# The recurrence gate's product dealt out between the attention's blocks, in a one-layer hybrid diffusion trunk

## The chip, the cores and the metric

One core of a Trainium2 chip runs the kernel. The time is device microseconds of one launch, the median of several runs. Lower is better.

## The reference

The reference is one layer of a latent diffusion trunk: 1024 latent tokens and 256 context tokens, width 1024, all in float32. Only what matters around the change is shown.

```python
z_q, z_k, z_v, z_dec, z_og, z_f, z_rx, z_rg = jnp.split(zl, IN_SPLITS, axis=-1)   # zl = hl @ w_in
q, k, v, la_f, la_b = gla_prepare(z_q, z_k, z_v, z_dec, w_dec, b_dec)
o_f, _ = gla_scan(q, k, v, la_f, s_f)
o_b_rev, _ = gla_scan(rev(q), rev(k), rev(v), rev(la_b), s_b)
...
h_f, h_b_rev = rglru_bidir(u, w_rg_a, b_rg_a, w_rg_x, b_rg_x, rg_lam, hf0, hb0)
...
y_gla = gla_norm_gate(o_gla, z_og, g_gla)
y_f = fourier_mix(z_f)
y_rg = h_rg * jax.nn.gelu(z_rg.astype(jnp.float32))
```

The layer's input is normalized and modulated into `hl` (the modulation's rows come from `w_ada`). One projection `w_in` gives the inputs of three parallel mixers: a gated linear attention in both directions over four heads, a 2-D Fourier mixing of `z_f`, and a convolution with a bidirectional linear recurrence whose output is multiplied by gelu of `z_rg`. The change is about that last product, `z_rg = hl @ w_in[:, 2080:2336]`. Behind the mixers come an output projection and a SwiGLU feed-forward.

## The kernel before, in words

Every large product is made of three float32r matmuls (`mm3`, L82 to L86): operands are split into a high half (a cast on ScalarE, ACT, L91) and a low half (a subtraction on VectorE, DVE, L92), and high x high, high x low and low x high are added in PSUM. `hl` is kept transposed, as 16 tiles. A transposed product such as `z_q`, `z_f` or `z_rg` is made in blocks of 128 output columns and halves of 512 tokens; each half needs eight steps of the contraction, 24 matmuls of 128x512. `z_T` makes halves one after the other; `z_steps` (L779) makes one half as a generator that stops after every second step of the contraction, so that a half is four pieces of six matmuls.

The attention works on two pairs of heads, `p` = 0 and 1. For each pair `kt_begin` (L507) starts the copy of `kT` with its halves exchanged, by DMAs from ACT's queue; `gla_states` (L579) makes the exponentials of the decays, the scaled keys `Kt`, their transposes `k_tr` on TensorE (PE), the products `kv` and from them the chunk states `St` on DVE (the `tt` and `St` instructions); it returns the last transpose as `mid`. Then `gla_block` (L620) is called for eight blocks of 128 tokens: the products `attn` on PE, masked on DVE (`am`), the products `o` on PE, their squares on ACT (`jk`), a scale `orst` on DVE and its power `ors` on GpSimd (POOL), and the scaled result `on` on ACT. It returns the last `attn` matmul as a mark.

Between the blocks stand pieces of other products. `queue` holds generators; `fill(n, mark)` (L792) takes n pieces from it and places them behind `mark` on PE. Before the change the queue holds q of pair 1 (`q_steps`, two halves) and f (`f_steps`, two blocks of columns with two halves each). The blocks of pair 0 take two pieces each, `gla_states(1)` three, the blocks of pair 1 one each, the last ones what is left. `rg_ctx` (L670) and `rg_gates` (L686) make the recurrence's gates: small matmuls `gate_ps` on PE, tanh and exponentials on ACT. `rg_scan` ends them with a square root on ACT and scans on DVE.

Behind the attention `z_rg` (L851, called in L919 and L920) makes the gate's product in one go, 96 matmuls, and evicts each quarter with a gelu on ACT into the tiles `yfr`. Then come eight steps of `ada_row` (L921): loads of `ada_raw` from `w_ada`, each multiplied and added to the tile `ada_acc` on DVE (L711). The first of these calls also ends the row before (two matmuls `row_ps`, two DVE instructions) and clears the next `ada_acc` on POOL and loads `b_ada` into it. Then come the weights `w_og` (loads, cast, subtraction), the recurrence's second half, the Fourier mixing, and the product `zn` of `w_og`.

What sets the order of the work: each engine runs its own list in order. The lists are made at compile time by a scheduler that runs a model of the time and takes, on each engine, the first in program order of those that are ready. Two things bind it: `issue_after(mark)` places what follows behind the mark on the same engine, and `in_order` (L1456) ties the first writes of all tiles of a memory pool to program order:

```python
NPG = 43
...
    for x, y in zip(first, first[1:]):
        if x is not y:
            tc.add_manual_dep(y, x.name, DATA, reason="memory in program order")

    in_order(names["pg"])
    in_order(names["hp"])
```

`pg` is a pool of 43 pages of 128x1024 floats in SBUF. `hl` takes 16 of them; weights (raw, high and low), `kT`, `Kt`, `St`, `qT`, `qTs`, `zf`, `yfr`, `on`, the recurrence's `tr`, `ti`, `a`, `rgc`, and each `ada_raw` and `ada_acc` take one page a tile. A load into a page waits for the last use of the tile that had it. PSUM has four banks `mm`, used by the pieces (`z`), by `o` and by `zn`, and four banks `aux`, used by the rest.

Of the kernel before, what the change touches and what calls it, by code (L numbers as in the profile page):

```python
# [13 lines left out]
AF = mybir.ActivationFunctionType  # L14
ALU = mybir.AluOpType

P = 128
# [10 lines left out]
C_Q, C_K, C_V, C_DEC, C_OG, C_F, C_RX, C_RG = 0, 256, 512, 1024, 1056, 1568, 1824, 2080  # L28
# [10 lines left out]
def tile_trunk(ctx: ExitStack, tc: tile.TileContext, A: dict):  # L39
# [9 lines left out]
    def pg(shape=(P, 1024), dt=F32, name="pg"):  # L49
        t = pool.tile(list(shape), dt, tag="pg", bufs=NPG, name=name)  # L50
        names["pg"].add(t.name)
        return t
# [180 lines left out]
    def w_T(c0):  # L233
        return split(w_T_load(c0), (P, KB, P))
# [193 lines left out]
    for p in range(2):  # L428
        ps = mm("zkc")
# [149 lines left out]
    def gla_states(p):  # L579

        gs = [gla_exp(p, d) for d in range(2)]
        St[p] = [pg((P, 8, P), name="St") for _ in range(2)]
        kn = {}
        for q in range(2):
            for d in range(2):
                kn[q, d], mid = gla_kT(p, d, q)
        tp = [None] * 2
        for q in range(2):
            for d in range(2):
                tp[d] = gla_kv(p, d, q, kn[q, d], gs[d], tp[d])  # L590
        return mid
# [4 lines left out]
    def z_q(p, h):  # L596
        if h == 0:
            qT.append(pg(name="qT"))
            qTs.append(pg(name="qTs"))
        hs = slice(h * 512, (h + 1) * 512)  # L600
        z_T(w_q[p], lambda ps, h: S.mul(qT[p][:, hs], ps, 0.125), (h,))
        exchange(qTs[p][:, hs], qT[p][:, hs])
# [17 lines left out]
    def gla_block(p, n):  # L620
        cs = slice(n * P, (n + 1) * P)
        if n % 4 == 0:
            gla_q(p, n // 4)
        am = hp((P, 2, P), name="am")
        at = [aux("attn")[:, 0:256].rearrange("p (d i) -> p d i", d=2) for _ in range(2)]
        for d in range(2):
            for h in range(2):
                mark = PE.matmul(at[h][:, d, :], Kt[p][d][R[h], cs], qx[p][h ^ d][R[h], cs], start=True, stop=True)
        for h in range(2):
            V.tensor_mul(am[:, h, :], at[h][:, 0, :], wmask)  # L630
            V.copy_predicated(am[:, h, :], imask, at[1 - h][:, 1, :])
        o = mm("o")
        for h in range(2):
            oc = o[:, h * P:(h + 1) * P]
            PE.matmul(oc, qx[p][h][:, cs], St[p][h][:, n, :], start=True, stop=False)
            PE.matmul(oc, am[:, h, :], vN[p][n // 4][:, n % 4, h * P:(h + 1) * P], start=False, stop=True)
        ss = sm("oss", 2)
        jk = pool.tile([P, P], mybir.dt.bfloat16, tag="jk", bufs=1, name="jk")
        for h in range(2):
            S.activation(jk, o[:, h * P:(h + 1) * P], AF.Square, accum_out=ss[:, h:h + 1])  # L640
        r = rstd(ss, P, "ors", 2)
        if n % 4 == 0:
            on[p][n // 4] = pg((P, 4, 256), name="on")
        for h in range(2):
            S.mul(on[p][n // 4][:, n % 4, h * P:(h + 1) * P], o[:, h * P:(h + 1) * P], r[:, h:h + 1])
        return mark
# [23 lines left out]
    def rg_ctx():  # L670
        tr, ti, a = (pg((P, 4, TC), name="rgc") for _ in range(3))
        for b in range(2):
            for d in range(2):
                rg_gate(tr[:, 2 * b + d, :], uTc[:, b, :], b, d, 0, TC)
                rg_gate(ti[:, 2 * b + d, :], uTc[:, b, :], b, d, 1, TC)
                rg_decay(a[:, 2 * b + d, :], tr[:, 2 * b + d, :], b, d)
            tv = ti[:, 2 * b:2 * b + 2, :]
            V.scalar_tensor_tensor(tv, tv, 1.0, uTc[:, b:b + 1, :].to_broadcast([P, 2, TC]), op0=ALU.add, op1=ALU.mult)
        rg_input(a, tr, ti)
        for b in range(2):  # L680
            for d in range(2):
                av, tv = a[:, 2 * b + d, :], ti[:, 2 * b + d, :]
                V.tensor_tensor_scan(fl(av, d), fl(av, d), fl(tv, d), 0.0, op0=ALU.mult, op1=ALU.add)
                V.tensor_copy(h0[:, 2 * d + b:][:, 0:1], av[:, (0 if d else TC - 1):][:, 0:1])
# [9 lines left out]
    def rg_scan(blk, d, part):  # L694
        a, tr, ti = part
        rg_input(a, tr, ti)
        V.tensor_tensor_scan(fl(a, d), fl(a, d), fl(ti, d), h0[:, 2 * d + blk:][:, 0:1], op0=ALU.mult, op1=ALU.add)
        if d == 0:
            hR.append(a)
        else:  # L700
            V.tensor_add(hR[blk], hR[blk], a)
# [51 lines left out]
    def ada_step(n=1):  # L753
        for _ in range(n):
            next(row_steps, None)
# [36 lines left out]
    def fill(n, mark):  # L792

        with tc.issue_after(mark.ins):
            while n and queue:
                if next(queue[0], queue) is queue:
                    queue.pop(0)
                else:
                    n -= 1

    def q_steps(p, h):
        hs = slice(h * 512, (h + 1) * 512)

        def ev(ps):
            S.mul(qT[p][:, hs], ps, 0.125)
            exchange(qTs[p][:, hs], qT[p][:, hs])
        return z_steps(w_q[p], h, ev)

    def f_steps(blk, h):
        return z_steps(w_f[blk], h, lambda ps: S.copy(zf[blk][:, h * 512:(h + 1) * 512], ps))  # L810

    mid = gla_states(0)
    z_q(0, 0)
    gates = pg((P, 8, P), name="gates")
    load(gates, A["gates"])
    with tc.issue_after(mid.ins):
        z_q(0, 1)
    rg_ctx()
    w_f = [w_T(C_F)]
    qT.append(pg(name="qT"))  # L820
    qTs.append(pg(name="qTs"))
    queue += [q_steps(1, 0), q_steps(1, 1)]
    for n in range(4):
        fill(2, gla_block(0, n))
        ada_step(0)
    w_f.append(w_T(C_F + P))
    zf = [pg(name="zf") for _ in range(2)]
    queue += [f_steps(0, 0), f_steps(0, 1)]
    for n in range(4, 8):
        fill(2, gla_block(0, n))  # L830
    kt_begin(1)
    mid = gla_states(1)
    queue += [f_steps(1, 0), f_steps(1, 1)]
    fill(3, mid)
    part = rg_gates(0, 0)
    for n in range(2):
        fill(1, gla_block(1, n))
    rg_scan(0, 0, part)
    for n in range(2, 4):
        fill(1, gla_block(1, n))  # L840
    w_rg = [w_T(C_RG)]
    part = rg_gates(0, 1)
    for n in range(4, 6):
        fill(1, gla_block(1, n))
    rg_scan(0, 1, part)
    for n in range(6, 8):
        fill(9, gla_block(1, n))
    w_rg.append(w_T(C_RG + P))

    yfr = [pg((P, 4, 256), name="yfr") for _ in range(4)]  # L850
    def z_rg(blk):  # L851
        def ev(ps, h):
            for j in range(2):
                act(yfr[2 * h + j][:, 2 + blk, :], ps[:, j * 256:(j + 1) * 256], AF.Gelu_apprx_tanh)
        z_T(w_rg[blk], ev)

    def y_rg(blk):
        for j in range(4):
# [57 lines left out]
            V.tensor_add(yfr[2][:, blk, 2 - q::2][:, ::-1], yc[:, m], ys[:, m])  # L916
        V.tensor_copy(yfr[2][:, blk, 0:1], cc[:, 0:1])

    z_rg(0)  # L919
    z_rg(1)  # L920
    ada_step(8)  # L921
    w_og = [w_N([(C_OG, 256)])]
    for d in range(2):
# [616 lines left out]
```

## Time and profile before

| what | value |
|---|---|
| median of 3 runs | 1119.17 us (1117.54 to 1119.43) |
| the profiled execution | 1119.34 us |
| its span, first to last instruction | 1116.6 us |
| PE busy with matmuls | 1079.7 us |
| DVE busy | 794.5 us |
| ACT busy | 506.4 us |
| POOL busy | 46.8 us |
| mean granted TensorE clock | 0.994 |

The 2.7 us between the time and the span lie around the first and the last instruction. Times in the rows are microseconds from the start of the span. The attention of pair 0 runs from about 186 to 239 us, that of pair 1 from about 247 to 287, `z_rg` from 276 to 300, and the product `zn` of `w_og` begins at 303. In a timeline row stand the start, the duration, the engine, the line and operation, the tiles (out<-in), the shapes and the number of instructions put together; in brackets the engine's idle time ahead of it and what ended that. An engine with a q (ACTq, SPq) is its sequencer issuing DMAs. Matmuls overlap one another, so the time that one takes is read from the distance of the starts.

### The profile page before, as it was taken

How to read it: one execution, taken by the hardware profiler on the slowest of the kernel's cores; microseconds unless marked ns; L12 is line 12 of the kernel's file. 1: busy time of each engine (PE TensorE's matmuls, PEld its weight loads, DVE VectorE, ACT ScalarE, POOL GpSimd, SP SyncE). 2: the span in 40 equal slices, each digit the busy share in tenths (PEclk: the TensorE clock that was granted, in tenths of full speed). 3: DMA queues.
4: the chain of work that ended last, by engine and by line, in shares of the span. 5: the costliest groups of instructions: out<-in, count | busy, mean ns of one | idle time of the engine just before them, and what ended most of it. 6: DMA issues, size and time to landing. Idle time of an engine off the chain costs nothing.

```text
span 1116.6 us, 15349 instructions
## 1 busy us (share of the span) xinstructions
PE 1079.7 (97%) x5696; PEld 902.2 (81%) x5696; DVE 794.5 (71%) x1394; ACT 506.4 (45%) x953; POOL 46.8 (4%) x64
## 2 busy tenths in 40 slices
PE   5999998999999999979999999999999999999997
PEld 3799896776789888858888888888888888888886
DVE  4375798476687445488897767887776569958694
ACT  4362765456453377684233332234232238554251
POOL 1000000113000010010000000000000000000100
PEclk9999999999999999989999999999999999999999
DMA  9913312121637232234443324633331578767572
GB/s 297 300 38 96 122 39 58 43 58 38 207 96 259 62 113 77 87 101 123 141 151 105 103 95 152 225 93 106 117 110 57 174 253 312 248 218 242 176 272 75
DMA packets 133411, 157.49 MB, mean 141 GB/s; under 512 B 8396, under 2 KB 88788, under 8 KB 133336
## 3 DMA queue, kind: packets, MB, share of 16 engines
q1 hardware_dynamic: 119400, 127.68, 36.4%
q10 hardware_dynamic: 13936, 28.84, 7.3%
q8 instruction: 44, 0.72, 0.3%
q14 instruction: 31, 0.25, 0.1%
HBM read 125.56 MB, written 28.57 MB: 138 GB/s over the span
## 4 chain that ended last, share of the span: by engine, by line
PE 89%; ACT 4%; DVE 3%; DMA 1%; issue 1%; POOL 1%; DVEq 0%; POOLq 0%; ACTq 0%
PE prod L86 12%; PE prod L84 12%; PE prod L85 12%; PE dn L84 6%; PE dn L86 6%; PE dn L85 6%; PE z L84 3%; PE z L85 3%; PE z L86 3%; PE o_ps L86 3%; PE o_ps L84 3%; PE o_ps L85 3%; PE zn L85 3%; PE zn L86 3%; PE zn L84 3%
## 5 line engine op out<-in xcount | busy, mean ns | idle before, releaser
L85 PE MATMUL dn<-dr,dl 128*128 128x512 f32 (+1 forms) x319 | 121.9, 382 | 0.0
L86 PE MATMUL dn<-dr,dl 128*128 128x512 f32 (+1 forms) x319 | 121.9, 382 | 0.0
L84 PE MATMUL dn<-dr,dl 128*128 128x512 f32 (+1 forms) x319 | 118.8, 382 | 0.0
L84 PE MATMUL prod<-a,b_hi 128*128 128x512 f32 x176 | 69.9, 397 | 4.2 <-ACT b_hi L91 4.2
L85 PE MATMUL zn<-w_lo,hl 128*128 128x256 f32 (+1 forms) x256 | 73.7, 291 | 0.0
L84 PE MATMUL zn<-w_hi,hl 128*128 128x256 f32 (+1 forms) x256 | 73.4, 290 | 0.0
L86 PE MATMUL zn<-w_hi,hl 128*128 128x256 f32 (+1 forms) x256 | 73.4, 289 | 0.0
L85 PE MATMUL prod<-a,b_hi 128*128 128x512 f32 x176 | 69.5, 395 | 0.0
L86 PEld LDWEIGHTS dn<-dr,dl 128*128 128x128 f32 x319 | 60.0, 188 | 11.6
L84 PEld LDWEIGHTS dn<-dr,dl 128*128 128x128 f32 x319 | 60.0, 188 | 11.5
L85 PEld LDWEIGHTS dn<-dr,dl 128*128 128x128 f32 x319 | 60.0, 188 | 11.6
L86 PE MATMUL prod<-a,b_lo 128*128 128x512 f32 x176 | 68.7, 395 | 0.6 <-DVE b_lo L92 0.6
L85 PE MATMUL prod<-s,wb_hi 128*128 128x512 f32 x176 | 68.5, 389 | 0.0
L84 PE MATMUL prod<-s,wb_hi 128*128 128x512 f32 x176 | 68.5, 389 | 0.0
L86 PE MATMUL prod<-s,wb_lo 128*128 128x512 f32 x176 | 68.4, 389 | 0.0
L84 PE MATMUL z<-hl,w_hi 128*128 128x512 f32 x160 | 63.0, 419 | 3.2 <-DVE hl L205 2.1
L85 PE MATMUL z<-hl,w_hi 128*128 128x512 f32 x160 | 63.9, 400 | 0.0
L1234 ACT CAST dl<-h 128x512 fp32r<-128x512 f32 x77 | 47.8, 621 | 34.2 <-issue 20.5
L86 PE MATMUL z<-hl,w_lo 128*128 128x512 f32 x160 | 63.1, 395 | 0.0
L1235 DVE TENSOR_TENSOR dl<-h,dl 128x512 fp32r<-128x512 f32 x77 | 53.0, 688 | 13.8 <-ACT dl L1234 13.7
L1167 ACT CAST b<-wf_raw 128x512 fp32r<-128x512 f32 x22 | 13.7, 623 | 102.4 <-PE prod L86 50.0
L1191 ACT ACTIVATE c<-c 128x512 f32<-128x512 f32 x22 | 13.9, 633 | 85.9 <-DVE c L1190 82.8
(376 smaller groups left out, 2805.5 us busy)
## 6 DMA issues: line engine op xcount, KB each, us to landing
ada_raw<-in_w_ada SPq DMA_DIRECT2D x48, 512.0 KB, 6.1
h<-hd SPq DMA_DIRECT2D x77, 256.0 KB, 4.3
wd_raw<-in_w_down SPq DMA_DIRECT2D x77, 256.0 KB, 5.1
wf_raw<-in_w_gate SPq DMA_DIRECT2D x28, 512.0 KB, 3.8
hd<-c ACTq DMA_DIRECT2D x52, 256.0 KB, 2.1
wf_raw<-in_w_up SPq DMA_DIRECT2D x22, 512.0 KB, 4.2
wraw<-in_w_in SPq DMA_DIRECT2D x12, 512.0 KB, 4.0
wo_raw<-in_w_out SPq DMA_DIRECT2D x8, 512.0 KB, 5.8
```

What stands on the lines that cost most here:

```text
L84: PE.matmul(out, lh, rh, start=start, stop=False)
L85: PE.matmul(out, lh, rl, start=False, stop=False)
L86: return PE.matmul(out, ll, rh, start=False, stop=stop)
L1167: S.copy(hi, u[:, 4:8])
L1191: S.activation(c21, c21, AF.Silu)
L1234: S.copy(t[:, 0, :], raw)
L1235: V.tensor_sub(t[:, 1, :], raw, t[:, 0, :].bitcast(F32))
```

## The change

The gate's product becomes 16 pieces (`rg_steps`, two blocks of columns with two halves of four pieces), evicted by plain copies into `yfr`, and joins the queue. The pieces move up: four of q stand behind the first pair's `mid`, ahead of `rg_ctx`; every block takes two, `gla_states(1)` four, and the last block what is left. The tiles `zf`, `yfr` and the gate's weights are made earlier accordingly. The gelu is done over the copied values behind the attention, in four instructions of 128x512. The calls `ada_step(0)` among the blocks are removed. The diff:

```diff
+    def rg_steps(blk, h):
+        def ev(ps):
+            for j in range(2):
+                S.copy(yfr[2 * h + j][:, 2 + blk, :], ps[:, j * 256:(j + 1) * 256])
+        return z_steps(w_rg[blk], h, ev)
+
     mid = gla_states(0)
     z_q(0, 0)
     gates = pg((P, 8, P), name="gates")
     load(gates, A["gates"])
-    with tc.issue_after(mid.ins):
-        z_q(0, 1)
-    rg_ctx()
-    w_f = [w_T(C_F)]
     qT.append(pg(name="qT"))
     qTs.append(pg(name="qTs"))
     queue += [q_steps(1, 0), q_steps(1, 1)]
+    with tc.issue_after(mid.ins):
+        z_q(0, 1)
+    fill(4, mid)
+    rg_ctx()
+    w_f = [w_T(C_F)]
+    zf = [pg(name="zf") for _ in range(2)]
+    queue += [f_steps(0, 0), f_steps(0, 1)]
     for n in range(4):
         fill(2, gla_block(0, n))
-        ada_step(0)
     w_f.append(w_T(C_F + P))
-    zf = [pg(name="zf") for _ in range(2)]
-    queue += [f_steps(0, 0), f_steps(0, 1)]
+    queue += [f_steps(1, 0), f_steps(1, 1)]
     for n in range(4, 8):
         fill(2, gla_block(0, n))
     kt_begin(1)
     mid = gla_states(1)
-    queue += [f_steps(1, 0), f_steps(1, 1)]
-    fill(3, mid)
+    fill(4, mid)
+    w_rg = [w_T(C_RG)]
+
+    yfr = [pg((P, 4, 256), name="yfr") for _ in range(4)]
+    queue += [rg_steps(0, 0), rg_steps(0, 1)]
     part = rg_gates(0, 0)
     for n in range(2):
-        fill(1, gla_block(1, n))
+        fill(2, gla_block(1, n))
     rg_scan(0, 0, part)
+    w_rg.append(w_T(C_RG + P))
+    queue += [rg_steps(1, 0), rg_steps(1, 1)]
     for n in range(2, 4):
-        fill(1, gla_block(1, n))
-    w_rg = [w_T(C_RG)]
+        fill(2, gla_block(1, n))
     part = rg_gates(0, 1)
     for n in range(4, 6):
-        fill(1, gla_block(1, n))
+        fill(2, gla_block(1, n))
     rg_scan(0, 1, part)
     for n in range(6, 8):
-        fill(9, gla_block(1, n))
-    w_rg.append(w_T(C_RG + P))
-
-    yfr = [pg((P, 4, 256), name="yfr") for _ in range(4)]
-    def z_rg(blk):
-        def ev(ps, h):
-            for j in range(2):
-                act(yfr[2 * h + j][:, 2 + blk, :], ps[:, j * 256:(j + 1) * 256], AF.Gelu_apprx_tanh)
-        z_T(w_rg[blk], ev)
+        fill(9 if n == 7 else 2, gla_block(1, n))
...
-    z_rg(0)
-    z_rg(1)
+    for j in range(4):
+        act(yfr[j][:, 2:4, :], yfr[j][:, 2:4, :], AF.Gelu_apprx_tanh)
     ada_step(8)
     w_og = [w_N([(C_OG, 256)])]
```

## Rows read from the trace of the kernel before

**Rows 1.** The page's first part: busy us, share of the span, instructions.

```profile
PE 1079.7 (97%) x5696; PEld 902.2 (81%) x5696; DVE 794.5 (71%) x1394; ACT 506.4 (45%) x953; POOL 46.8 (4%) x64
```

**Rows 2.** Stretches: start:end, length; busy PE, PEld, DVE, ACT, POOL; clock, DMA, GB/s.

```profile
190.00:200.00 10.00, 6.73 (x28) 5.65 (x29) 8.29 (x17) 8.56 (x14) 0.00 (x0) 0.83 0.01 2
200.00:240.00 40.00, 40.00 (x243) 32.00 (x243) 20.45 (x56) 18.87 (x61) 6.49 (x7) 1.00 0.22 53
240.00:276.00 36.00, 33.18 (x203) 23.11 (x199) 27.07 (x68) 25.02 (x57) 7.06 (x7) 1.00 0.12 34
```

**Rows 3.** PE's timeline ahead of the first block's o.

```profile
191.21 0.46 PE L628 MATMUL attn<-la,Kt 64*128 64x128 f32 x2 [1.51 <-DVE tt L573]
...
192.34 0.49 PE L628 MATMUL attn<-qT,Kt 64*128 64x128 f32 x2 [0.45 <-DVE am L630]
...
194.66 0.77 PE L635 MATMUL o<-St,qT 128*128 128x128 f32 x2 [1.61 <-DVE St L559]
...
196.50 0.63 PE L85 MATMUL z<-hl,w_hi 128*128 128x512 f32 x1
```

**Rows 4.** PE's timeline, the last two matmuls of z_rg.

```profile
299.55 0.39 PE L85 MATMUL z<-hl,w_hi 128*128 128x512 f32 x1
299.77 0.39 PE L86 MATMUL z<-hl,w_lo 128*128 128x512 f32 x1
```

**Rows 5.** PE's timeline, waits from 240 to 277 us.

```profile
244.30 2.81 PE L653 MATMUL gate_ps<-uT,gates 128*128 128x512 f32 x6 [1.06 <-DVE tt L573]
...
268.04 0.49 PE L636 MATMUL o<-vN,am 128*128 128x128 f32 x2 [0.37 <-DVE am L631]
...
273.65 0.49 PE L636 MATMUL o<-vN,am 128*128 128x128 f32 x2 [0.42 <-DVE am L631]
...
276.25 0.50 PE L84 MATMUL z<-hl,w_hi 128*128 128x512 f32 x1 [1.02 <-ACT on L645]
```

**Rows 6.** The turn to pair 1: ACT's and PE's timelines, Kt's landing, its products.

```profile
221.79 0.58 ACT L810 COPY zf<-z 128x512 f32<-128x512 f32 x1
221.79 1.12 ACTq L231 DMA_DIRECT2D Kt<-kT  x2
...
231.96 1.03 PE L549 MATMUL k_tr<-cm,Kt 128*128 128x128 f32 x8
...
Kt<-kT ACTq DMA_DIRECT2D x4, 256.0 KB, 3.7
...
L534 DVE TENSOR_TENSOR Kt<-Kt,ek 128x512 f32<-128x512 f32 x4 | 2.7, 684 | 0.0
```

**Rows 7.** Weights of f and gate: DVE's and ACT's timelines, landing of wraw.

```profile
195.14 1.22 DVE L92 TENSOR_TENSOR w_lo<-wraw,w_hi 128x1024 fp32r<-128x1024 f32 x1
...
259.68 1.07 ACT L91 CAST w_hi<-wraw 128x1024 fp32r<-128x1024 f32 x1
...
DMA to landing us min/median/max: 3.7/4.0/9.9
```

**Rows 8.** Behind the attention: the timelines of SP, DVE and PE.

```profile
275.05 5.23 SPq L70 DMA_DIRECT2D ada_raw<-in_w_ada  x3
287.55 0.24 SPq L70 DMA_DIRECT2D ada_acc<-in_b_ada  x1
...
285.68 0.17 DVE L119 TENSOR_SCALAR orst<-oss 128x2 f32<-128x2 f32 x1 [1.23 <-ACT jk L640]
...
290.42 10.53 DVE L711 SCALAR_TENSOR_TENSOR ada_acc<-ada_raw,s,ada_acc 128x1024 f32<-128x1024 f32 x8
...
301.82 2.36 DVE L92 TENSOR_TENSOR w_lo<-wraw,w_hi 128x1024 fp32r<-128x1024 f32 x2 [0.88 <-ACT w_hi L91]
...
300.00 3.59 PE L653 MATMUL gate_ps<-uT,gates 128*128 128x512 f32 x8
303.03 1.04 PE L84 MATMUL zn<-w_hi,hl 128*128 128x256 f32 x4
```

**Rows 9.** SP's waits from 120 to 380 us: total, times, longest.

```profile
SPq L70 <- DVE ti L665: 16.1, 2, 12.6
```

## The prediction

> **What bounds the kernel now.** I read the page's first part, then the table of stretches, then PE's timeline through the attention, then the timelines of ACT, DVE and SP for what stands around it. The page gives PE 97% of the span [rows 1]. The stretches [rows 2] say where PE is not busy: from 190 to 200 us (6.73 of 10.00, at a mean granted clock of 0.83) and from 240 to 276 (33.18 of 36.00); from 200 to 240 it is full. So the change can win only what PE loses in such stretches, and the sum below is one of PE's gaps: closed, left, and new.
>
> The losses by row. Ahead of the first block PE waits 1.51, 0.45 and 1.61 us, and right behind the third wait a 512-column matmul shows 0.63 us [rows 3] where later ones show 0.39 [rows 4]: the lower of the clock's two levels, 1.2 GHz, after three waits in a row. A clock of 0.83 over 10 us [rows 2] costs 10 x 0.17 = 1.7 us. Together 3.57 + 1.7 = 5.3 us. In the second pair's attention PE waits 1.06, 0.37, 0.42 and 1.02 us [rows 5]: 2.9 us. All that is to be won is 8.2 us, 0.7%.
>
> **The change part by part**, against the profiled execution's own 1119.34 us (span 1116.6 and 2.7 around it; 0.2 above the median of 1119.17).
>
> Work. The 16 pieces are the 96 matmuls that z_rg runs from 276.25 to 299.77 [rows 4, 5], at 0.23 us apart some 22 us; none is removed. Queue and slots match: q, f and gate have 8 + 16 + 16 = 40 pieces, and the fills take 4 + 16 + 4 + 14 and the last 2. ACT gets eight copies of 128x256 more. The nearest row is the zf copy of twice the size, 0.58 us [rows 6], so at most 4.7 us, in an attention where ACT is busy 25 of 36 us [rows 2]. The gelu goes from eight halves to four wholes, no dearer: 4 x 0.58 = 2.3 us. Both are costed at nothing: no PE instruction waits for the copies but through a bank, and the gelus fall in a wait for loads (below); without that cover they would cost 2.3 us. ada_step(0) issues nothing, so its removal is free. The number of DMAs is unchanged.
>
> First gap. Four q pieces (24 matmuls, 5.5 us) now stand behind z_q(0,1), just where PE lost 5.3 us. But memory is given in program order, and qT, qTs of pair 1 now stand ahead of the rgc tiles: their eviction and two exchange DMAs come first on ACT's queue, so rg_ctx's chain on ACT starts some 5 us later, with everything that waits for its scratch pages. The first f weights are split by 195.14 + 1.22 [rows 7]. They had the two pages of w_q(0), which now go to qT and qTs; raw, hi and lo come instead from what gla_q and rg_ctx release, between 193 and 202 by my count, plus a load of 4.0, a cast of 1.07 and a subtraction of 1.22 [rows 7]: about 205. f pieces are wanted from the third block, about 203. Ends: 5.3 won, or nothing. I take **-3.4**, nearer the full win, as f would be some 2 us late.
>
> Second pair's gaps. Two pieces a block instead of one put 8 x 1.37 us more matmuls where 2.9 us of waits stand. Ends -2.9 and 0; **-2.6**, since the first pair's blocks, with two pieces each, run from 200 to 240 with PE full [rows 2].
>
> The turn between the pairs. Now the exchange into Kt of pair 1 is issued at 221.79, right behind the first zf copy on ACT, and the first transposes of it (k_tr) run at 231.96 [rows 6], with z pieces over these 10.2 us. In program order Kt's pages stand behind zf[0]. In the changed order zf[1] stands ahead of Kt, and it is written by f(1,0), the last piece of block 7; so exchange, exponentials, products and transposes begin when PE has run out of pieces, and the next four are placed behind the last k_tr. The chain alone: copy 0.58, issues 1.12, landing 3.7, two products of 0.68 [rows 6]: 6.8 us. Under it lie o products (four pairs a block, at most 0.49 each [rows 5]: 2.0) and, if the order puts them there, the matmuls of rg_gates(0,0) (3.6, as those at 300.00 [rows 8]). Ends 0 and 7, the last with the clock's fall; I take **+3.0**, between what is left with both covers (1.2) and with one (4.8).
>
> Behind the attention. What lies under z_rg? On DVE eight ada steps of 1.28 us without a break from 290.42, on SP b_ada at 287.55 and the loads behind it; only then come w_lo at 301.82 and the first zn at 303.03 [rows 8]. The last block's orst is at 285.68, so 17.4 us pass from there to zn, with 14 us of z over them and 3.0 of gates(1,0), from 300.00 [rows 8]. In the change z is over when block 7 is: its last two pieces stand right behind that block's attn. The chain of loads and DVE steps gets no shorter, and can't come much earlier, since each load takes a page: SP waits 16.1 us in two waits for DVE's last use of ti [rows 9]. I count pages, of 43: at block 5 of pair 1 the change holds hl 16, on 4, yfr 4, zf 2, w_rg 2, Kt 2, St 2, tr, ti and a 3, and one each of hR, uT, gates, ada_acc, qT, la, vN: 42. yfr's four are there during the attention now, not behind it. So at most three ada_raw are ahead until block 7 lets go of its pages, as the three of 275.05 were [rows 8]. Good end: b_ada (2.9 us, 287.55 to 290.42) and three steps (3.8) are done by then; of the 15.5 us from 287.55 to 303.03 there are 8.8 left, less 1 for the end of the pieces and 3.0 for the gates: 4.8. Bad end: no head start, 17.4 - 3.0 = 14.4. I take **+7.0**, nearer the good end, as three pages do come free before. From zn on the order is as before, so the loss is final.
>
> The sum: -3.4 - 2.6 + 3.0 + 7.0 = **+4.0**: 1123.3 us against 1119.34, or 1123.2 against the median.
>
> A rule on this. The rows show PE full where z pieces stand between blocks, and not full where few do [rows 2]. The Trainium skill (Perfetto Trace Analysis, Optimization Strategy) says that a kernel whose busiest engine changes over time may gain by interleaving its regimes; by that alone the two gains stay and the two losses don't, 1113.3. The same section says that bubbles that keep coming back can mean that there is no room for the next tile; SP's waits for pages [rows 9] agree with that one.
>
> **The rivals.**
> A, the other side, faster: the order made at compile time takes row, b_ada, ada steps and w_og's halves into the second pair's attention. Place: the first zn behind the last gate piece. It decides where w_lo is ready within 3.0 us of that piece. For it: yfr no longer holds up row, acc and ada_raw in the order of memory, and DVE is idle 9 of the 36 us from 240 to 276 [rows 2], nearly the 10.3 us of the steps. Against: the page count. Price: -3.4 - 2.6 + 1.0 (the turn well covered) = -5.0: **1114.2** against the median.
> B, slower still: both new waits near their bad ends, 5 and 14, with the two gains: +13: **1132**. For it: the eight steps stand ahead of w_lo in program order; against: three loads at 275.05 were early [rows 8].
> C, the change does not do what it says: the gate's weights aren't ready for the first pieces (the cast of w_rg(0) is placed as late as 259.68 [rows 7]), PE takes what it has, and z is still done behind the attention, over the loads, as before. Gains and losses then stay small: **1119.2**.
>
> **How the numbers follow.** A measurement of this kernel can tell about 0.2% (2.2 us) from no change. Forecast 0.40, B 0.09, A 0.33, C 0.18. Slower: forecast and B but for a hundredth: 0.48. Faster: A but for the hundredth that falls short of 2.2 us: 0.32. Same: C and these two: 0.20. The predicted time is the forecast's, 1123.2, with a range of its own from 1121.5 to 1128. For 8 in 10 I go from 1112.5, where both gains are whole and the new waits small, to 1129.5, which leaves out most of B.
>
> **What would show it.** Right: from 190 to 200 PE is full at a clock of 1.00; no wait above 0.5 us in pair 1's blocks; PE idle between the last o of pair 0 and k_tr, with the exchange issued right behind the second zf copy; behind the last z matmul PE idle for several us ahead of the first zn, which waits for w_lo, while DVE does the eight ada steps. Wrong: ada steps among the blocks of pair 1 and zn within 3 us of the last z (then A); z matmuls alone behind the last attn (then C); PE idle for over 3 us ahead of the first f piece (then the first gain was mis-sized).

## The result, and the profile after

The changed kernel takes **1130.79 us** (median of four runs, 1129.48 to 1131.36) against 1119.16 before: a ratio of 1.011 with a 95% interval from 1.0097 to 1.0122. It is slower by 11.6 us; 4.0 had been forecast. The profiled span grew from 1116.6 to 1127.7 us.

The page's first part, columns as in [rows 1]:

```profile
PE 1078.9 (96%) x5696; PEld 902.5 (80%) x5696; DVE 796.9 (71%) x1394; ACT 508.2 (45%) x957; POOL 41.9 (4%) x64
```

PE has no more work than in [rows 1], and DVE and ACT only 2.4 and 1.8 us more. The added time is mostly waiting. The stretches of the changed kernel, columns as in [rows 2], say where:

```profile
190.00:200.00 10.00, 9.15 (x72) 7.21 (x71) 6.71 (x25) 7.76 (x18) 0.00 (x0) 1.00 0.32 81
200.00:240.00 40.00, 32.73 (x186) 27.39 (x186) 20.68 (x47) 24.48 (x69) 5.83 (x8) 0.92 0.19 46
240.00:276.00 36.00, 36.00 (x210) 26.64 (x207) 21.57 (x49) 17.83 (x43) 4.72 (x4) 0.99 0.12 34
...
300.00:326.00 26.00, 16.91 (x93) 13.65 (x92) 19.24 (x19) 16.97 (x19) 1.09 (x3) 0.80 0.47 169
```

Against [rows 2], the first and the third stretch are what was hoped for: PE rises from 6.73 to 9.15 us, with the clock back at 1.00, and from 33.18 to 36.00, which is full. The second stretch was full before and has lost 7.27 us; the last one has lost 9.09, at a mean clock of 0.80. Two new waits have taken the place of the old ones.

**The first new wait, the turn between the pairs.** ACT's, PE's and DVE's timelines, to set beside [rows 6]:

```profile
228.55 0.58 ACT L810 COPY zf<-z 128x512 f32<-128x512 f32 x1 [0.30 <-PE z L86]
228.56 0.47 ACTq L231 DMA_DIRECT2D Kt<-kT  x1
229.33 0.47 ACTq L231 DMA_DIRECT2D Kt<-kT  x1
...
232.47 0.66 PE L549 MATMUL k_tr<-cm,Kt 128*128 128x128 f32 x4 [3.29 <-DVE Kt L537]
237.11 2.40 PE L549 MATMUL k_tr<-cm,Kt 128*128 128x128 f32 x10 [3.98 <-DVE Kt L534]
...
235.76 1.29 DVE L534 TENSOR_TENSOR Kt<-Kt,ek 128x512 f32<-128x512 f32 x2
```

The exchange into Kt is issued with a zf copy, as in [rows 6], but it is now the last copy of f(1,0), with no piece left behind it. PE stands 3.29 + 3.98 = 7.27 us while DVE makes Kt. In the second wait DVE is busy all the time, but not with Kt alone: the exchange lands 3.4 us after its issue, by 232.8, and the exponentials are there by 233.9, yet Kt's products begin at 235.76, behind four products of qT and two of St. So some 2 us of it are DVE's order.

**The second, behind the attention.** The timelines of SP, POOL, ACT, DVE and PE, to set beside [rows 8]; the last line is SP's wait on the memset, in total, times, longest:

```profile
287.36 2.49 SPq L70 DMA_DIRECT2D ada_raw<-in_w_ada  x3
297.26 0.24 SPq L70 DMA_DIRECT2D ada_acc<-in_b_ada  x1
297.56 2.49 SPq L70 DMA_DIRECT2D ada_raw<-in_w_ada  x5
300.14 1.01 SPq L70 DMA_DIRECT2D wraw<-in_w_in  x2
...
294.85 1.49 POOL L121 TENSOR_TENSOR ors<-orst,mhalf 128x2 f32<-128x2 f32 x2 [1.67 <-DVE orst L119]
296.29 0.95 POOL L706 MEMSET ada_acc<- 128x1024 f32 x1
...
308.45 1.04 ACT L91 CAST w_hi<-wraw 128x1024 fp32r<-128x1024 f32 x1 [10.15 <-DMA wraw<-in_w_in]
...
295.40 0.17 DVE L119 TENSOR_SCALAR orst<-oss 128x2 f32<-128x2 f32 x1 [0.63 <-ACT jk L640]
298.85 10.53 DVE L711 SCALAR_TENSOR_TENSOR ada_acc<-ada_raw,s,ada_acc 128x1024 f32<-128x1024 f32 x8
309.53 1.22 DVE L92 TENSOR_TENSOR w_lo<-wraw,w_hi 128x1024 fp32r<-128x1024 f32 x1
...
295.19 1.88 PE L722 MATMUL row_ps<-ada_acc,cm 128*128 128x512 f32 x4
296.90 3.60 PE L653 MATMUL gate_ps<-uT,gates 128*128 128x512 f32 x8
309.55 1.22 PE L84 MATMUL zn<-w_hi,hl 128*128 128x256 f32 x4 [9.05 <-ACT w_hi L91]
...
SPq L70 <- POOL ada_acc L706: 7.3, 1, 7.3
```

The last z matmul starts at 294.96; row_ps and eight gates follow, and then PE waits 9.05 us. What it waits for is the chain of [rows 8], in the same order: the last block's rstd (its power) on POOL, the memset behind it, the b_ada load behind that, and then two branches of equal length, five ada_raw and two wraw loads until w_hi at 308.45, and eight steps on DVE until w_lo at 309.53. From the last orst at 295.40 to zn it is 14.2 us long, and 5.1 us of row_ps and gates lie over it. SP stood on the memset 7.2 us in the kernel before as well. Only then some 14 us of the gate's product lay over it.

The granted clock is at the lower of its two levels behind this wait. PE's timeline of the changed kernel, and then of the kernel before, in the same product:

```profile
311.19 0.41 PE L86 MATMUL zn<-w_hi,hl 128*128 128x256 f32 x1
311.40 0.41 PE L84 MATMUL zn<-w_hi,hl 128*128 128x256 f32 x1
```

```profile
306.44 0.28 PE L84 MATMUL zn<-w_hi,hl 128*128 128x256 f32 x1
306.56 0.28 PE L85 MATMUL zn<-w_lo,hl 128*128 128x256 f32 x1
```

The matmuls are 0.21 us apart instead of 0.12, until 315.4. Those 5.9 us hold work that takes about 2.9 us at full clock (5.85 / 2), so by this estimate 2.9 us go there.

### The profile page after: what moved, and what is told of

Same layout as the page of the kernel before. It is cut to its first block, busy times and chain, and to the rows that moved or that the text cites. A ratio compares the mean times of both kernels' runs of the same rounds, so it can differ in the third digit from the quotient of the medians.

```text
span 1127.7 us, 15366 instructions
## 1 busy us (share of the span) xinstructions
PE 1078.9 (96%) x5696; PEld 902.5 (80%) x5696; DVE 796.9 (71%) x1394; ACT 508.2 (45%) x957; POOL 41.9 (4%) x64
## 4 chain that ended last, share of the span: by engine, by line
PE 89%; DVE 4%; ACT 3%; DMA 2%; issue 1%; POOL 0%; ACTq 0%; DVEq 0%; POOLq 0%; SPq 0%
PE prod L86 12%; PE prod L84 12%; PE prod L85 12%; PE dn L84 6%; PE dn L86 6%; PE dn L85 6%; PE z L84 3%; PE z L85 3%; PE z L86 3%; PE o_ps L84 3%; PE o_ps L86 3%; PE o_ps L85 3%; PE zn L84 3%; PE zn L85 3%; PE zn L86 3%; DMA wraw<-in_w_in 1%
## 5 line engine op out<-in xcount | busy, mean ns | idle before, releaser
L84 PEld LDWEIGHTS zn<-w_hi,hl 128*128 128x128 f32 x256 | 49.7, 195 | 10.7 <-ACT w_hi L91 9.9
```

Source lines behind the costliest of these rows:

```text
L84: PE.matmul(out, lh, rh, start=start, stop=False)
```

## Experiments

Each kernel was timed in three rounds beside the kernel before, on the same chip. After each "Result" stand its median, that of before, and the ratio with its interval. Rows come from one profiled execution, which can lie up to 2 us off the median (e1 above it; e6, e7 and e11 below).

### Undo one wait at a time

**e1_zf_early**: one column of zf[1] is cleared by POOL ahead of pair 0's last blocks, so that the page of zf[1] is taken there and Kt's pages, next in program order, need not wait for f(1,0)'s copies.

```diff
+    G.memset(zf[1][:, 0:1], 0.0)
     queue += [f_steps(1, 0), f_steps(1, 1)]
     for n in range(4, 8):
```

> One instruction is added to the changed kernel: a POOL memset of one column of zf[1], ahead of the pair 0 blocks 4 to 7, so that zf[1]'s place in the order of memory no longer hangs on f(1,0), the last piece of block 7. Theory (order of memory): the exchange into Kt of pair 1 is issued several us ahead of the second zf copy, the first k_tr follows the last z of block 7 within 1 us, PE's idle time between 228 and 240 us (3.29 + 3.98 us and a granted clock of 0.92 in 200 to 240) goes; the time falls by 6 to 8 us, to 1123 to 1125. Rival (pieces spent too early): PE has nothing to do at the turn whatever the order of memory, since ACT and DVE are late; then Kt starts earlier but k_tr does not come more than 2 us earlier against the last z, and the time stays within 2 us of 1130.8. The 9 us ahead of the first zn stay in both.

Result: 1120.84 against 1118.15, 1.0019 [1.0007, 1.003]. The exchange goes out at 219.10, k_tr has one wait of 0.81 us left, and the other wait stays (zn's is 9.46). The order of memory made the wait, and the gain is 10.0 us where 6 to 8 were expected. ACT's and PE's timelines:

```profile
219.10 0.47 ACTq L231 DMA_DIRECT2D Kt<-kT  x1
...
232.11 0.55 PE L549 MATMUL k_tr<-cm,Kt 128*128 128x128 f32 x3 [0.81 <-ACT kn L551]
```

**e2_wog_first**: the first w_og tile ahead of the eight steps.

```diff
-    ada_step(8)
     w_og = [w_N([(C_OG, 256)])]
+    ada_step(8)
```

> In the changed kernel the loads and halves of w_og stand ahead of the eight ada steps. Theory (cover taken away): the first zn waits for the loads and the DVE steps ahead of w_og in program order; with w_og first it starts within 1 to 4 us of the end of the gates(1,0) matmuls instead of 9.4, the clock does not fall there, and the time falls by 7 to 12 us, to 1119 to 1124; the ada steps run beside zn. Rival (pages): w_og's loads get their pages only when the last block is done in either order, so that zn moves by the 10.5 us of the steps at most in part: a gain of 2 to 5 us, 1126 to 1129. The turn's idle time (3.3 + 4.0 us) stays in both.

Result: 1120.46 against 1118.15, 1.0023 [1.0008, 1.0037]. zn follows the gates at once; the turn is as before the edit; a part is lost later, where PE waits 3.15 us for DVE's zfold, at 339.00. Stretches:

```profile
300.00:326.00 26.00, 25.93 (x187) 22.87 (x186) 21.61 (x24) 18.75 (x22) 1.45 (x4) 1.00 0.47 170
326.00:336.00 10.00, 8.73 (x61) 8.04 (x59) 9.96 (x17) 2.09 (x2) 0.10 (x1) 1.00 0.66 204
336.00:346.00 10.00, 6.67 (x32) 6.33 (x33) 7.92 (x26) 3.87 (x6) 0.00 (x0) 0.83 0.90 326
```

So each wait is worth about 10 us of the time (1130.79 less 1120.84, and less 1120.46; by the ratios 10.2 and 9.7). That is more than their lengths of 7.3 and 9.1 us, and the clock is down behind both.

**e3_both**: both edits.

> Both edits in the changed kernel. Theory: the two idle times are the whole loss and independent: the gains of the two single edits add up to within 2 us, 13 to 20 us together, and the time comes to 1111 to 1117, ahead of the kernel before (1119.2), since the two gains of the change (first gap, waits in pair 1's blocks, 8.2 us of idle before) are kept. Rival: one idle time grows when the other is closed (PE comes to the end of the attention earlier, while loads and pages come when they come): the sum falls short by over 4 us and the time stays at or above 1119.

Result: 1116.37 against 1118.15, 0.998 [0.9971, 0.999]. Faster than the changed kernel and, by 0.2%, than the kernel before, but the two gains don't add: 14.4 of 20.3 us. The time is the theory's, the shortfall of 5.9 us the rival's. PE is 10.0 us ahead of the kernel before in the middle of zn (its 51st matmul starts at 302.85 and at 312.83), and then:

```profile
326.00:336.00 10.00, 6.85 (x41) 6.59 (x40) 8.65 (x27) 0.44 (x1) 0.00 (x0) 0.74 0.97 357
336.00:346.00 10.00, 9.97 (x51) 8.86 (x51) 6.64 (x14) 4.08 (x7) 0.00 (x0) 0.74 0.46 161
```

**e4_q_ahead**: from the kernel before, only the q pieces ahead of rg_ctx; zf's tiles are made earlier, as in the change, blocks 4 to 7 of pair 0 get one piece each, and the turn and z_rg stay.

```diff
-    with tc.issue_after(mid.ins):
-        z_q(0, 1)
-    rg_ctx()
...
     queue += [q_steps(1, 0), q_steps(1, 1)]
+    with tc.issue_after(mid.ins):
+        z_q(0, 1)
+    fill(4, mid)
+    rg_ctx()
...
     for n in range(4, 8):
-        fill(2, gla_block(0, n))
+        fill(1, gla_block(0, n))
```

> The kernel before with the change's first part alone: four q pieces behind the first mid, ahead of rg_ctx; blocks 4 to 7 of pair 0 take one piece each instead of two, so that Kt's order of memory and z_rg stay as before. Theory: PE's idle time from 189 to 195 us and the low clock behind it (5.3 us) go but for 1 us, and the four pieces fewer in blocks 4 to 7 open at most 1 to 2 us there: 1115 to 1117. Rival: rg_ctx started later on ACT holds up blocks 0 to 2 and the f weights, and the gain is lost there: 1119 or more.

Result: 1116.69 against 1118.15, 0.9983 [0.9973, 0.9992]. The first gap closes (PE 9.28 of 10.00), but the thinner blocks open waits of 1.55 and 0.68 us around the turn (the wait of 1.06 in [rows 5] becomes 1.29), and one of 1.91 us ahead of Z_ps, the first Fourier product, is new. 1.5 us (1118.15 less 1116.69) is what is left of the 4.

### What is in the last wait

**e5_gelu_alone**: from the kernel before, the product where it was, evicted by copies, and the gelu once over each tile behind both blocks.

```diff
-                act(yfr[2 * h + j][:, 2 + blk, :], ps[:, j * 256:(j + 1) * 256], AF.Gelu_apprx_tanh)
+                S.copy(yfr[2 * h + j][:, 2 + blk, :], ps[:, j * 256:(j + 1) * 256])
...
+    for j in range(4):
+        act(yfr[j][:, 2:4, :], yfr[j][:, 2:4, :], AF.Gelu_apprx_tanh)
```

> The kernel before, with one part of the change alone: the gate's product stays where it was, but its eight halves leave PSUM by plain copies and the gelu then runs once over each of the four tiles. Theory (the gelu's form costs nothing, as the prediction put it): the four gelus fall while ScalarE waits for the wraw load behind the attention (10.53 us of loads and VectorE steps there), zn still starts near 303 and the time is within 1.5 us of the kernel before. Rival (the four gelus stand ahead of w_hi and the tanh gates on ScalarE and push them back): 2.3 to 4 us slower than before, with zn 2 us or more later.

Result: 1122.1 against 1118.26, 1.0033 [1.0021, 1.0044]. The time is the rival's, but not by its mechanism. DVE's and PE's timelines, and then DVE's in the kernel before:

```profile
289.12 1.28 DVE L711 SCALAR_TENSOR_TENSOR ada_acc<-ada_raw,s,ada_acc 128x1024 f32<-128x1024 f32 x1 [1.92 <-DMA ada_acc<-in_b_ada]
297.50 0.94 DVE L859 TENSOR_TENSOR yfr<-yfr,a 128x256 f32<-128x256 f32 x2 [7.10 <-ACT yfr L77]
298.37 5.24 DVE L711 SCALAR_TENSOR_TENSOR ada_acc<-ada_raw,s,ada_acc 128x1024 f32<-128x1024 f32 x4
...
307.99 0.39 PE L85 MATMUL zn<-w_lo,hl 128*128 128x256 f32 x1 [3.80 <-DVE w_lo L92]
```

```profile
289.74 0.76 DVE L859 TENSOR_TENSOR yfr<-yfr,a 128x256 f32<-128x256 f32 x2 [2.66 <-ACT yfr L77]
```

A gelu over both blocks can't run until the second block is there. The multiplication of the first block by the recurrence (L859) stands on DVE ahead of the ada steps, waits 7.10 us for it, and seven of the eight steps, and w_lo behind them, wait too. w_hi was only 1.15 us later (301.90 against 300.75).

**e6_loads_first**: in the changed kernel, the loads of w_og alone ahead of the steps.

```diff
+    raw_og = w_N_load([(C_OG, 256)])
     ada_step(8)
-    w_og = [w_N([(C_OG, 256)])]
+    w_og = [w_N_split(raw_og)]
```

> The changed kernel with the loads of the first w_og tile alone ahead of the eight adaptive-row steps; its split into w_hi and w_lo stays behind them in the program. It asks what made the last gap of the changed kernel: the place of the two wraw loads on SP's queue, or the eight VectorE steps of 1.3 us ahead of the w_lo split. Loads theory: the gap ahead of zn (9.05 us in the changed kernel) goes, and the time falls to 1119 to 1123, as when the loads and the split were both moved (1120.5). VectorE rival: w_hi comes early but w_lo still ends behind eight steps of 10.5 us in all, so that the gap stays at 6 us or more and the time at 1126 to 1131.

Result: 1122.05 against 1118.26, 1.0037 [1.002, 1.0055]. The gap goes, but the run doesn't separate the two theories: with its data early, the first w_lo split was placed ahead of the steps as well (DVE L92 at 299.63, the first step at 300.77).

**e10_pool_load**: in the changed kernel, b_ada on POOL's queue, so that SP doesn't stand on the memset.

```diff
-        load(acc[0:1, :], A["b_ada"][:, c0:c0 + D])
+        G.dma_start(acc[0:1, :], A["b_ada"][:, c0:c0 + D])
```

> The changed kernel with the load of b_ada alone moved from SP's queue to GpSimd's, right behind the memset that it waits for. In the changed kernel SP stands 7.3 us on that memset (it ends at 297.25, behind the last rstd on GpSimd) with five ada_raw and two wraw loads queued behind it. Loads theory of the last gap: with SP free the wraw loads go out some 7 us earlier, w_hi comes near 301, the gap of 9.05 us ahead of zn falls below 4 us, and the time is 1122 to 1127. VectorE theory: the eight steps of 1.3 us still cannot begin before the memset and the bias have landed, 298 to 300, at least seven of them stand ahead of the first w_lo on VectorE, and the gap stays at 7 us or more though w_hi is early: 1128 to 1132.

Result: 1129.62 against 1117.33, 1.0106 [1.0091, 1.0121]. POOL's, ACT's, DVE's and PE's timelines:

```profile
297.91 0.54 POOL L707 DMA_DIRECT2D ada_acc<-in_b_ada  x1 [0.30 <-POOL ada_acc L706]
...
304.59 1.04 ACT L91 CAST w_hi<-wraw 128x1024 fp32r<-128x1024 f32 x1 [5.91 <-DMA wraw<-in_w_in]
303.07 9.21 DVE L711 SCALAR_TENSOR_TENSOR ada_acc<-ada_raw,s,ada_acc 128x1024 f32<-128x1024 f32 x7 [3.93 <-DMA wraw<-in_w_in]
305.69 0.93 PE L84 MATMUL zn<-w_hi,hl 128*128 128x256 f32 x4 [4.81 <-ACT w_hi L91]
...
313.47 0.58 PE L85 MATMUL zn<-w_lo,hl 128*128 128x256 f32 x1 [3.76 <-DVE w_lo L92]
```

w_hi comes 3.9 us earlier and nothing is won, since w_lo still stands behind seven steps. Part of zn's wait has only moved behind its first matmuls. But the edit held up the steps as well: on POOL's queue b_ada took 5.1 us to land, to 303.0, and the steps begin at 303.07 in place of 298.85. (The row names the wraw load as what ended their wait, but a step doesn't read wraw.) So the run shows that an early w_hi alone wins nothing, not what w_lo costs with the steps in their place.

**e14_no_memset**: in the changed kernel, the first step writes its product in place of adding it to a cleared tile. The bias b_ada is left out of the rows.

```diff
-        G.memset(acc, 0.0)
-        load(acc[0:1, :], A["b_ada"][:, c0:c0 + D])
...
+            if k == 0:
+                V.tensor_scalar_mul(acc, raw, s32[:, k, 0:1])
+            else:
+                V.scalar_tensor_tensor(acc, raw, s32[:, k, 0:1], acc, op0=ALU.mult, op1=ALU.add)
```

> The changed kernel with the first adaptive-row step writing its product instead of adding it to a cleared tile: no memset on GpSimd, and no load of b_ada; the bias of the rows is left out of what is computed. Theory (the last gap hangs on the memset, which stands behind the last block's rstd on GpSimd, and holds the loads on SP and the steps on VectorE alike): loads by 291, steps on VectorE from 293 to 298 on between the last blocks' work, w_lo near 305 in place of 309.5, the gap ahead of zn 3 to 6 us in place of 9.05, the time 1123 to 1128. Rival (the pages that the loads go into, or VectorE's own work up to 298.8, hold them as long): the gap 8 us or more, 1129 to 1132. The rest of the program's order shifts a little with it, so the gap itself decides, not the last microsecond of the time.

Result: 1126.01 against 1117.33, 1.0072 [1.0055, 1.0089]. DVE's and PE's timelines:

```profile
298.81 0.75 DVE L710 TENSOR_SCALAR ada_acc<-ada_raw,s 128x1024 f32<-128x1024 f32 x1
...
304.78 0.74 PE L84 MATMUL zn<-w_hi,hl 128*128 128x256 f32 x4 [4.16 <-ACT w_hi L91]
309.99 0.58 PE L85 MATMUL zn<-w_lo,hl 128*128 128x256 f32 x1 [4.47 <-DVE w_lo L92]
```

The time lies where the theory put it, the rows don't: zn waits 4.16 us for w_hi and 4.47 for w_lo, 8.63 together, which is the rival's gap, and the gap was to decide. The steps begin at 298.81, as in the changed kernel (298.85). In front of them on DVE stand row_ps's product and the multiplications that wait for the gelus, and those end with the attention. So the memset is one of several ties. This run also separates the two branches: w_hi is cast 4.8 us earlier (303.69) with the steps in their place, and w_lo behind them holds PE almost as long. The waits are 0.4 us shorter than 9.05; where the rest of the 4.8 us of time is won is not traced.

### Is the last wait only lost cover?

**e18_half_behind**: in the changed kernel, the gate's second block (8 of the 16 pieces) behind the attention again, its gelu from PSUM as before; one piece goes to each block of pair 1. In the program the order of loads, memset and steps stays.

```diff
-    queue += [rg_steps(1, 0), rg_steps(1, 1)]
...
     for j in range(4):
-        act(yfr[j][:, 2:4, :], yfr[j][:, 2:4, :], AF.Gelu_apprx_tanh)
+        act(yfr[j][:, 2, :], yfr[j][:, 2, :], AF.Gelu_apprx_tanh)
+    for h in range(2):
+        def ev1(ps, h=h):
+            for j in range(2):
+                act(yfr[2 * h + j][:, 3, :], ps[:, j * 256:(j + 1) * 256], AF.Gelu_apprx_tanh)
+        for _ in z_steps(w_rg[1], h, ev1):
+            pass
```

> The changed kernel with the second block of the gate's product (8 of the 16 pieces, some 11 us of PE) run behind the attention again, as before; one piece then goes to each block of pair 1. The loads, the memset and the VectorE steps stay in their order. Cover theory of the last gap: these stand 12 to 14 us long behind the attention in either kernel, and only the product ahead of them hid them; with 11 us of it back the gap ahead of zn falls from 9 us to 0 to 2, the clock stays up, the turn's wait stays, and the time is 1118 to 1122. Rival (the gap comes from what the dealt-out copies and gelus do to ScalarE and VectorE): 1126 to 1131.

Result: 1117.3 against 1118.1, 0.999 [0.9981, 1.0]. 11 us of product are enough: zn has no wait that the timeline shows, though the turn's 7 us are all there. The stretches, and DVE's timeline:

```profile
200.00:240.00 40.00, 32.73 (x182) 27.41 (x181) 20.53 (x46) 24.69 (x70) 5.83 (x8) 0.93 0.20 47
300.00:326.00 26.00, 24.41 (x165) 20.81 (x164) 19.84 (x24) 21.25 (x24) 1.09 (x3) 1.00 0.34 102
...
289.77 1.27 DVE L711 SCALAR_TENSOR_TENSOR ada_acc<-ada_raw,s,ada_acc 128x1024 f32<-128x1024 f32 x1
292.02 0.17 DVE L119 TENSOR_SCALAR orst<-oss 128x2 f32<-128x2 f32 x1 [0.97 <-ACT jk L640]
```

That it is the cover alone is not shown. The compiled order moved with the product: the memset (286.20) and the first step (289.77) now come ahead of the last block's orst at 292.02, and from that orst to zn at 301.74 the chain is 9.7 us long, not 14.2. Half of the copies and of the late gelus, which are the rival's cause, went with the edit too.

### Where the lead goes, and the best version

**e7_ada_late**: both edits of e3, and all ada steps behind the Fourier calls.

```diff
-    ada_step(8)
     w_og = [w_N([(C_OG, 256)])]
...
-    ada_step(1)
     w_og.append(w_N([(C_OG + 256, 256)]))
...
-    ada_step(7)
+    ada_step(8)
     z_og(0, range(8))
-    ada_step(9)
+    ada_step(8)
...
     z_og(1, range(4))
+    ada_step(1)
```

> The changed kernel with both repairs together (one-column memset of zf[1]; w_og's loads and split first), and all adaptive-row steps moved behind the two Fourier calls: eight ahead of the products by w_og[0], eight behind them, the last one behind the first half of those by w_og[1]. The two repairs together measured 1116.4 where their single gains would add to about 1110.5; theory: the missing 6 us went to VectorE, which was full from 310 to 337 us, with 3.2 us of waits ahead of Z_ps, 1.1 us more ahead of 326 us and a granted clock of 0.74 from 326 to 346 us. With some 13 us of steps taken out of that stretch PE should stay busy there and the time come to 1108 to 1113. Rival (the steps are then late for the columns and rows that the output product and the norm need, or their loads come behind w_out's): 1115 to 1122, with new waits between 350 and 400 us.

Result: 1119.54 against 1118.26, 1.0011 [0.9997, 1.0025]. PE holds its lead through the Fourier part and then waits for the late steps, as the rival has it; PE's timeline:

```profile
360.05 3.57 PE L716 MATMUL col_ps<-cm,ada_acc 128*128 128x1 f32 x16 [2.47 <-DVE ada_acc L711]
...
404.43 0.51 PE L84 MATMUL o_ps<-wo_hi,yh 128*128 128x512 f32 x1 [2.06 <-ACT yh L989]
```

**e8_og_late**: both edits of e3, and the second w_og tile behind the second Fourier call.

```diff
-    w_og.append(w_N([(C_OG + 256, 256)]))
     fourier(zf[1], 1)
+    w_og.append(w_N([(C_OG + 256, 256)]))
```

> The two repairs together, with only the second w_og tile (its loads and two splits of 1.22 us on VectorE) moved behind the second Fourier call. Theory: it takes 2.4 us from VectorE's full stretch, and the two loads from the stretch at 326 to 336 us in which the DMA share was 0.97: 1113 to 1116. Rival (VectorE's order is not what PE waits for there, or the second tile is then late): 1116 to 1119, with the waits at 326 to 336 us unchanged.

Result: 1116.22 against 1118.26, 0.9977 [0.9967, 0.9987], between the two. PE is now full from 326 to 336 us (10.00), but waits 1.77 us on DVE ahead of it and 2.06 at 400.87, as in e7; the time is e3's.

**e11_f1_pair1**: the changed kernel with f(1) left in pair 1, and w_og first.

```diff
     w_f.append(w_T(C_F + P))
-    queue += [f_steps(1, 0), f_steps(1, 1)]
     for n in range(4, 8):
-        fill(2, gla_block(0, n))
+        fill(1, gla_block(0, n))
     kt_begin(1)
     mid = gla_states(1)
+    queue += [f_steps(1, 0), f_steps(1, 1)]
...
```

> The change with two differences: f's second block stays in pair 1, as before (so no piece of pair 0 writes zf[1], and four blocks of pair 0 get one piece each instead of two), and the first w_og tile's loads and split stand ahead of the adaptive-row steps. Theory (the two waits are all that the change costs, and where f's second block is computed is what tied Kt to ScalarE's copies): no gap ahead of k_tr, none ahead of zn, and 1112 to 1117, at or a little under the 1116.4 of the two repairs by memset and order, since the pieces saved from pair 0 leave one wait of some 2 us there but more cover in pair 1. Rival (a lead made in the attention is given back behind it, whatever made it, as the output product is held by its own loads and splits): 1115.5 to 1119, with PE ahead by 8 us or more at 300 us and by under 3 us at 420 us.

Result: 1119.21 against 1117.33, 1.0013 [1.0004, 1.0023]. The rival again: PE waits 3.15 us on zfold at 334.00, and of 6.8 us of lead in zn (its 51st matmul) 1.9 are left at the end of the output product. In all three, as I read it, the steps that lost their cover behind the attention want DVE somewhere else; but e4, where they kept it, has a wait on zfold too (1.91 us).

**e18b_half_early** is e18 with e1's memset. **e18c_half_f1** is e18 with f(1) in pair 1 (blocks 0 to 3 of either pair get two pieces, blocks 4 to 7 one), without the memset.

> The same, and the one-column memset of zf[1] that unties Kt from ScalarE's copies. Cover theory: both waits are gone while the adaptive-row steps keep their old place under a product, so VectorE is not overfull in the Fourier part: PE ahead of the kernel before by 7 to 11 us at 330 us, and 1107 to 1113 if that lead lives. Rival (a lead made here is given back between 380 and 500 us, as in the three kernels with both waits repaired, which end 0.7 to 1.7 us ahead of before whatever their lead of 8 to 13 us at 300 us): 1115 to 1118.

> The changed kernel with f's second block in pair 1 as before, the gate's first block dealt out in pair 1 too, and its second block behind the attention as before: nothing of the memset, no reordered load. It has one piece a block in half of each pair. Cover theory: no gap ahead of k_tr over 2 us and none ahead of zn, waits of 1 to 2 us in the blocks with one piece; 1110 to 1115 if the lead lives. Rival (given back later): 1115 to 1118.

Results: **e18b 1112.24 against 1118.1, 0.9941 [0.9926, 0.9956]**; e18c 1114.07, 0.9958 [0.9943, 0.9974]. Here the lead lives. The 32 transposes of y, as the views of that tile give them (count, shortest, median and longest in ns, first and last start), in the kernel before, in e3 and in e18b:

```profile
L984 PE MATMUL y_tr<-cm,on x32: 271/273/307, 361.7 to 446.1; 128*128 128x128 f32 x32
```

```profile
L988 PE MATMUL y_tr<-cm,on x32: 270/272/309, 361.9 to 443.2; 128*128 128x128 f32 x32
```

```profile
L993 PE MATMUL y_tr<-cm,on x32: 270/273/307, 354.7 to 439.0; 128*128 128x128 f32 x32
```

The last of them is 7.1 us early in e18b and 2.9 in e3. e18b's waits ahead of zn are 0.85 and 0.52 us:

```profile
294.42 0.74 PE L84 MATMUL zn<-w_hi,hl 128*128 128x256 f32 x4 [0.85 <-ACT w_hi L91]
295.68 0.39 PE L85 MATMUL zn<-w_lo,hl 128*128 128x256 f32 x1 [0.52 <-DVE w_lo L92]
```

## Why the prediction was right or wrong

The direction and the places were right, the size was not: 1123.2 forecast, 1112.5 to 1129.5 given, 1130.79 measured. Point by point:

- **First gap, -3.4 taken.** Right, a little low. The stretch lost 3.27 us of waiting and some 1.7 of clock before, 0.85 and nothing after: 4.1 won. The f weights were not late.
- **Pair 1's gaps, -2.6 taken.** Right: 2.82 us in [rows 2], none after. Its signs came too: no wait in pair 1's blocks. (They get 11 more pieces, 16 where 5 stood, not 8; this changes neither end.)
- **The turn, +3.0 taken between 0 and 7. The first step that failed.** It measured 7.27 us of waiting, above the bad end even without its clock. The mechanism is as told, pages in program order with zf[1] ahead of Kt, and e1 confirms it. What failed is "between what is left with both covers and with one": neither cover was there. rg_gates(0,0) was not placed in the turn (its first matmul is at 249.10), and the o products were over at 229.2, 0.6 us behind the start of the copy. I had put in as a middle what was an order that I had not read. The chain was too short as well, 6.8 us where copy to second k_tr took 8.6 (228.55 to 237.11): DVE's products of qT and St, ahead of Kt's, were not in it.
- **Behind the attention, +7.0 taken between 4.8 and 14.4. The second.** It measured 9.05 us. "b_ada and three steps are done by then" failed: three ada_raw came early, as counted (287.36), but no step ran early. The bias waits for the memset, which stands on POOL behind the last block's rstd, and DVE's own queue is taken until then (e14). All eight steps began at 298.85. So the good end had no reason behind it. The bad end, 17.4 - 3.0, was wrong in both numbers: the chain took 14.2 us, and its cover, with row_ps, was 5.1. Nor were 2.9 us the time of b_ada: in [rows 8] DVE stood behind the multiplication that waits for a gelu (289.74, in e5's rows), and in e5 the load ends a wait 1.5 us after its issue (287.66 to 289.12). The place was right: zn waits behind the last z matmul, on w_hi, which came with w_lo.
- **The clock, left out of the second term.** The sum counted the lower clock only where the old waits cost it (1.7 us) and as part of the turn's bad end. Behind the 9.05 us it takes some 2.9 more. Behind the turn's wait, ten k_tr take 2.40 us where eight took 1.03 in [rows 6], 1.1 us more. With both the terms are -4.1 - 2.8 + 7.3 + 1.1 + 9.1 + 2.9 = +13.5, against 11.1 of the two spans; the 2.4 between them are not traced to a row.
- **The gelu, costed at nothing.** The price was wrong where it can be seen alone: e5 costs 3.8 us. The prediction priced the four activations on ACT (2.3 us if uncovered). The price is on DVE, whose queue stands still behind the multiplication that waits for the gelu. In the changed kernel those multiplications end as the steps begin, at 298.8, so they are one of the ties of the last wait (e14) and not added to it.
- **Rival B** (1132, both waits near their bad ends) came within 1.2 us and had 0.09. Its reason, the eight steps ahead of w_lo, was read right; the three early loads were held against it, and no step ran early with them. That the time is so close is in part luck: B had 5 and 14 us for the two waits, which measured 7.3 and 9.1 with the clock's 1.1 and 2.9 beside them.

Of the rule in the prediction: the Trainium skill (Perfetto Trace Analysis, Optimization Strategy) says that interleaving regimes may help where the busiest engine changes. By that alone it was to be 1113.3; here it was 1130.79. The trace agrees with the rule once half of the product stays behind as cover and Kt is untied (e18b, 1112.24).

Open remains why a lead of 7 to 10 us is lost in so many places. DVE is full there (17.90 of 18.00 us from 318 to 336 in e11), but in the kernel before it is as full from 326 to 336 (9.93 of 10.00) and PE is full beside it; and e8, which takes work from that stretch, has a ratio of 0.9977 where e3 has 0.998, which is no difference. That DVE's order sets it is argued from the waits, not shown by a run that changes it alone. Open as well is how much of the wait behind the attention is lost cover and how much the later place of memset and steps: e18 changes both.

## What to carry to other kernels

Before work is moved into gaps, list what runs under it where it stands now: loads, a memset, another engine's steps. That list is a chain with a length, and the length less what is left above it is the price; here moving all lost 12 us, moving half and leaving the other half as cover came out even (e18, 0.999), and with Kt untied as well it won 6 (e18b). A middle between two ends is worth nothing unless some row makes it likely: read the queue orders (POOL's and DVE's too) until one end falls, and add the clock behind every new wait of several us.

## What was not expected of the hardware

- **A long wait of PE cost more than its length.** Behind the 9.05 us wait the clock was at the lower of its two levels, 1.2 of 2.4 GHz, for 5.9 us (matmuls of 128x256 0.21 us apart, not 0.12); the same came in e1 behind 9.46 us (a mean clock of 0.79 from 300 to 326 us). Behind single waits of 0.5 to 1.2 us it stayed at 1.00 (e18b, 276 to 326 us).
- **A load's landing varied with what stood in line.** The wraw loads, 4.0 us in the middle in [rows 7], took 8.3 and 9.2 us here: issued from 300.14 on, the first landed by 308.45, behind five ada_raw loads of 512 KB that had been issued in the 3 us before. In the kernel before, the same two, behind five such loads as well, took 9.9 us, the longest of [rows 7].
- **The same small load took longer on POOL's queue.** b_ada, 4 KB, landed 5.1 us after its issue there (e10); on SP's queue steps that read it ran 1.5 and 1.6 us after its issue (e5 and the changed kernel).
